# Differential attention in a two-layer hybrid block: where the difference of the two softmax maps is formed

## The chip, the cores and the metric

The kernel runs on one core of a Trainium2 chip. A core has five engines with queues of their own: TensorE (PE, matrix products into PSUM), VectorE (DVE), ScalarE (ACT, activations), GpSimd (POOL) and SyncE (SP, which issues the DMAs). Each engine takes its instructions strictly in the order in which they were written into its queue, and semaphores make them wait for one another. The metric is the device time of one execution in microseconds, the median of several runs.

## The reference

Two layers, each with three mixers side by side (neighbourhood attention, differential attention, a bidirectional state space model), an output projection, and a gated MLP with a convolution. The change touches differential attention alone. There are 4 heads, and each has two softmax maps, of which the second is taken off with a learned factor:

```python
def diff_attend(q, k, v, lam):
    s = jnp.einsum('bqhmd,bkhmd->bhmqk', q, k).astype(jnp.float32) * DF_HEAD_DIM ** -0.5
    p = jax.nn.softmax(s, axis=-1)
    a = p[:, :, 0] - lam * p[:, :, 1]
    return jnp.einsum('bhqk,bkhe->bqhe', a.astype(v.dtype), v)
```

Each output row of a head is then divided by its root mean square (`finish` in `diff_mixer`), so a common factor of a row drops out but for the small constant in that norm. 1024 latent tokens read 1280 keys (latent and context); in layer 0 the 256 context tokens are queries too and read the 256 context keys.

## The kernel before

All values are float32. The big projections split their operands into two float32r halves and use three products instead of one float32 product. Differential attention is the generator `df_stream` (L716). Its unit is 128 queries of one head: 40 units in layer 0 (of which 8 have 256 keys and the rest 1280) and 32 in layer 1, 72 in all. A unit has three steps.

`scores` (L743): for each of the two maps three float32r products of queries and keys into PSUM (L759; 512, 512 and 256 keys). DVE copies each out into the map's tile `e` and takes its maximum (L760), ACT applies the exponential with the row sum accumulated into `sums` (L764). The maps are not divided by their sums: the ratio rho = -lambda * sum0 / sum1 is formed (L767 on DVE, L768 on POOL), and POOL forms e0 + rho * e1 in two passes over 1280 columns (L770, L772).

`turn` (L778): PE transposes the result in blocks of 128 x 128 (L786), four of them into one PSUM bank, and ACT copies each bank into a tile `at` (L787). There are 10 blocks in a unit of 1280 keys, 656 in all.

`values` (L791): the transposed blocks are the moving side of the products with the values (L801), whose stationary side has 64 columns. Every fourth query tile the row norm follows (L812 to L827), and the result goes to DRAM in `ydd`.

The stream runs one unit ahead: `scores` of unit i stands in front of `turn` of unit i-1. Its first ten steps are interleaved with the projection of the neighbourhood values (`proj_tm`, L849), the rest with neighbourhood attention (`natt`, L1069) and with the modulation products of the next layer (`ada_native`, L325). The loop at L864 deals these out in proportion. On top of that a scheduler, which goes by its own estimate of how long things take, decides the order in each engine's queue when the program is built. The program text is therefore no guide to the order, and the tables below are.

After the stage the output projection (`outproj`, L1655) reads `ydd` back from DRAM.

In the names: `s` and `t` are PSUM tiles of scores and of transposed blocks, `qst` and `ks` queries and keys, `cs` the constants (with the identity in it), `dfv` the values, `o` the output in PSUM. Names with n in front (`ns`, `nt`, `nsb`, `npt`, `nk`, `nqs`) belong to neighbourhood attention.

Of the kernel before, what the change touches and what calls it, by code (L numbers as in the profile page):

```python
# [10 lines left out]
F32 = mybir.dt.float32  # L11
F32R = mybir.dt.float32r
ACTF = mybir.ActivationFunctionType
ALU = mybir.AluOpType
# [21 lines left out]
NB = 12  # L36
XN = (0, 0)
PD = 0
DG = lambda b, qt, hh: True

V_CW = 0
V_CB = V_CW + 40
# [38 lines left out]
def hybrid_kernel(ctx, tc, xin, cc, w_ada, bada, gmf, w_in, w_dt, w_out, w_up, w_dn, vec, cst, rope, nab, out):  # L81
    nc = tc.nc
    V, S, G, PE, SP = nc.vector, nc.scalar, nc.gpsimd, nc.tensor, nc.sync
# [49 lines left out]
    dr = ctx.enter_context(tc.tile_pool(name="dr", bufs=1, space=DRAM))  # L133
# [52 lines left out]
    ident = C(C_ID)  # L186
# [328 lines left out]
    def mixer(l):  # L515
# [9 lines left out]
        lam = keep.tile([128, 1], F32, name="lam")  # L525
# [62 lines left out]
        with phase(f"sw{l}") as sp:  # L588
          dte = sp.tile([128, NT, 16], F32, name="dte")
          tot = sp.tile([128, NT, 16], F32, name="tot")  # L590
          with phase(f"dtp{l}") as p:
# [13 lines left out]
            for t in range(NT):  # L605
                PE.matmul(pd_[:, t * 16:(t + 1) * 16], dt32[:, t * 128:(t + 1) * 128], C(C_I16, 16, 32),
                          start=True, stop=True)
            sm = lambda nm: p.tile([128, NT, 16], F32, name=nm)
            x0, ax, e, u, lu, um, eq = [sm(nm) for nm in ("sx", "sax", "se", "su", "slu", "sum_", "seq")]
            V.tensor_tensor(out=x0, in0=pd_[:, 0:160].rearrange("p (t c) -> p t c", t=NT),  # L610
                            in1=vc[:, l, V_DTB:V_DTB + 16].unsqueeze(1).to_broadcast([128, NT, 16]), op=ALU.add)
# [35 lines left out]
          if True:  # L647
            p = sp
# [67 lines left out]
        def df_stream():  # L716
            ks = {}
            units = [(b, qt, hh) for b in range(2) for qt in range(10 if full else 8) for hh in range(2)]
            held = {}
            qst = {}  # L720
            po = {}
            dgs = {}

            def load_k(b):
                t = (p if b == 0 else ksp[0]).tile([128, 4, T], F32R, tag="ks", name="ks")
                for j in range(4):
                    SP.dma_start(out=t[32 * j:32 * j + 32].bitcast(F32),
                                 in_=qkd[l][1, b, j // 2].rearrange("(m d) t -> d m t", m=4))
                ks[b] = t

            def load_q(b, qt):
                t = p.tile([128, 4, 128], F32R, tag="qst", name="qst", bufs=2)
                for j in range(4):
                    SP.dma_start(out=t[32 * j:32 * j + 32].bitcast(F32),
                                 in_=qkd[l][0, b, j % 2, :, qt * 128:qt * 128 + 128]
                                 .rearrange("(m d) t -> d m t", m=4))
                qst[b, qt] = t

            def keys(qt):
                k0, nk = (0, T) if qt < 8 else (SEQ, CTX)  # L740
                return k0, nk, [(c, min(512, nk - c)) for c in range(0, nk, 512)]

            def scores(b, qt, hh):  # L743
                if b not in ks:
                    load_k(b)
                if (b, qt) not in qst:
                    load_q(b, qt)
                k0, nk, kch = keys(qt)
                es = []
                if hh == 0 and qt % 4 == 0:  # L750
                    dgs[b, qt // 4] = p.tile([128, 2, 8], F32, tag="sums", name="sums", bufs=3)
                sm, u = dgs[b, qt // 4], qt % 4 * 2 + hh
                for m in range(2):
                    mi = hh * 2 + m
                    e = p.tile([128, T], F32, tag="e", name="e", bufs=EB)
                    mx = p.tile([128, 4], F32, tag="mx", name="mx", bufs=4)
                    for ci, (c, n) in enumerate(kch):
                        s_ = pst("s", 2)[:, :n]
                        PE.matmul(s_, qst[b, qt][:, mi], ks[b][:, mi, k0 + c:k0 + c + n], start=True, stop=True)  # L759
                        V.tensor_scalar(out=e[:, c:c + n], in0=s_, scalar1=1.0, scalar2=None,  # L760
                                        op0=ALU.mult, op1=ALU.max, accum_out=mx[:, ci:ci + 1])
                    nm = p.tile([128, 1], F32, tag="nm", name="nm", bufs=4)
                    V.tensor_reduce(out=nm, in_=mx[:, 0:len(kch)], axis=AX.X, op=ALU.max, negate=True)  # L763
                    act(out=e[:, 0:nk], in_=e[:, 0:nk], func=ACTF.Exp, bias=nm, accum_out=sm[:, m, u:u + 1])  # L764
                    es.append(e)
                rho = p.tile([128, 1], F32, tag="rho", name="rho", bufs=4)
                V.reciprocal(out=rho, in_=sm[:, 1, u:u + 1])  # L767
                G.tensor_scalar(out=rho, in0=rho, scalar1=sm[:, 0, u:u + 1], scalar2=lam, op0=ALU.mult, op1=ALU.mult)  # L768
                if DG(b, qt, hh):
                    G.tensor_scalar(out=es[1][:, 0:nk], in0=es[1][:, 0:nk], scalar1=rho, scalar2=1.0,  # L770
                                    op0=ALU.mult, op1=ALU.mult)
                    G.tensor_tensor(out=es[0][:, 0:nk], in0=es[0][:, 0:nk], in1=es[1][:, 0:nk], op=ALU.add)  # L772
                else:
                    V.scalar_tensor_tensor(out=es[0][:, 0:nk], in0=es[1][:, 0:nk], scalar=rho,
                                           in1=es[0][:, 0:nk], op0=ALU.mult, op1=ALU.add)
                held[b, qt, hh] = es[0]

            def turn(b, qt, hh):  # L778
                k0, nk, kch = keys(qt)
                e0 = held[b, qt, hh]  # L780
                ac = []
                for c, n in kch:
                    at = p.tile([128, n], F32, tag=f"at{n}", name="at", bufs=n // 128)
                    tp = pst("t", 2)
                    for i in range(n // 128):
                        PE.transpose(tp[:, i * 128:(i + 1) * 128], e0[:, c + i * 128:c + (i + 1) * 128], ident)  # L786
                    S.copy(out=at[:, :n], in_=tp[:, :n])  # L787
                    ac.append(at)
                held[b, qt, hh] = ac

            def values(b, qt):  # L791
                g0, gn = (qt // 4 * 4, 4) if qt < 8 else (8, 2)
                qi = qt - g0
                if qi == 0:
                    po[b] = pst("o", 1)
                k0, nk, kch = keys(qt)
                nkt = nk // 128
                for kt in range(nkt):
                    for hh in range(2):
                        hd = 2 * b + hh  # L800
                        PE.matmul(po[b][64 * hh:64 * hh + 64, qi * 128:(qi + 1) * 128],  # L801
                                  dfv[:, k0 // 128 + kt, hd * 64:(hd + 1) * 64],
                                  held[b, qt, hh][kt // 4][:, (kt % 4) * 128:(kt % 4 + 1) * 128],
                                  start=(kt == 0), stop=(kt == nkt - 1))
                if qi < gn - 1:
                    return
                n = gn * 128
                c0 = g0 * 128
                pv = po[b][:, :n]
                tl = lambda nm, dt=F32: p.tile([128, 512], dt, tag=nm, name=nm, bufs=1)[:, :n]  # L810
                sq, oh = tl("dsq"), tl("doh", F32R)
                act(out=sq, in_=pv, func=ACTF.Square)  # L812
                dg = p.tile([128, 8], F32, tag="dg", name="dg", bufs=2)
                s0 = dgs[b, qt // 4][:, 0, 0:2 * gn]
                V.scalar_tensor_tensor(out=dg[:, 0:2 * gn], in0=s0, scalar=64 * EPS, in1=s0, op0=ALU.mult, op1=ALU.mult)
                pm = pst("t", 2)[:, :n]
                PE.matmul(pm, C(C_BD64), sq, start=True, stop=False)
                for i in range(gn):
                    for hh in range(2):
                        PE.matmul(pm[64 * hh:64 * hh + 64, i * 128:(i + 1) * 128],  # L820
                                  dg[:, 2 * i + hh:2 * i + hh + 1].to_broadcast([128, 64]), ident,
                                  start=False, stop=(i == gn - 1))
                rstd(sq, pm, 1.0 / 64, oh.bitcast(F32), bias=0.0)
                V.scalar_tensor_tensor(out=sq, in0=pv, scalar=sub, in1=sq, op0=ALU.mult, op1=ALU.mult)
                split(oh, sq, sq, G)
                SP.dma_start(out=ydd[l][2 + b, 0, :, c0:c0 + n], in_=oh.bitcast(F32))
                SP.dma_start(out=ydd[l][2 + b, 1, :, c0:c0 + n], in_=sq)  # L827

            for i in range(len(units) + 1):
                if i < len(units):  # L830
                    scores(*units[i])
                if i > 0:
                    b, qt, hh = units[i - 1]
                    turn(b, qt, hh)
                    if hh:
                        values(b, qt)
                yield
# [1043 lines left out]
```

## Time and profile before

| | |
|---|---|
| three runs | 3574.5, 3579.18, 3580.07 us (median 3579.18) |
| the profiled execution | 3568.3 us, its span 3566.3 us |
| PE busy | 3274.8 us (92%), 17970 records |
| weight loads on PE | 2579.0 us (72%) |
| POOL busy | 1797.8 us (50%), 1391 instructions |
| DVE busy | 2272.8 us (64%) |
| ACT busy | 1514.2 us (42%) |

The differential stage of layer 0 lies at about 606 to 905 us of the span and that of layer 1 at about 2440 to 2730 us. A PE instruction shows as two kinds of record: a weight load (PEld, the stationary side) and a matmul (PE, the moving side). A transposition has one record of each kind (656 for 656 blocks), a float32 product has two of each (1312 of L801 for 656 products), a float32r product one. Successive matmuls overlap in the trace: one of 128 columns lasts some 270 ns, but the next starts much earlier. What an instruction costs PE is read from start to start, not from its duration.

### The profile page before, as it was taken

How to read it: one execution, taken by the hardware profiler on the slowest of the kernel's cores; microseconds unless marked ns; L12 is line 12 of the kernel's file. 1: busy time of each engine (PE TensorE's matmuls, PEld its weight loads, DVE VectorE, ACT ScalarE, POOL GpSimd, SP SyncE). 2: the span in 40 equal slices, each digit the busy share in tenths (PEclk: the TensorE clock that was granted, in tenths of full speed). 3: DMA queues.
4: the chain of work that ended last, by engine and by line, in shares of the span. 5: the costliest groups of instructions: out<-in, count | busy, mean ns of one | idle time of the engine just before them, and what ended most of it. 6: DMA issues, size and time to landing. Idle time of an engine off the chain costs nothing. (4 is left out here: it accounts for less than half of the span.)

```text
span 3566.3 us, 50227 instructions
## 1 busy us (share of the span) xinstructions
PE 3274.8 (92%) x17970; PEld 2579.0 (72%) x17970; DVE 2272.8 (64%) x4074; ACT 1514.2 (42%) x2641; POOL 1797.8 (50%) x1391
## 2 busy tenths in 40 slices
PE   7998998899888999998998998998998979999899
PEld 3876776667767887887786876776766757777677
DVE  6635875667485555556768745884674666776753
ACT  4233433778263233333335433344774533333343
POOL 2136663667244444544554226663674455555444
PEclk8999999999999999999999999998999989999999
DMA  8355444753722222225443245447555422222633
GB/s 294 105 189 180 133 124 134 193 153 107 260 90 68 89 91 79 89 86 183 145 133 110 84 145 198 125 131 190 169 172 194 152 71 89 92 93 99 240 114 118
DMA packets 328473, 491.24 MB, mean 138 GB/s; under 512 B 28320, under 2 KB 182048, under 8 KB 327968
## 3 DMA queue, kind: packets, MB, share of 16 engines
q1 hardware_dynamic: 328224, 488.03, 43.0%
q8 instruction: 142, 2.33, 0.3%
q14 instruction: 107, 0.88, 0.1%
HBM read 349.25 MB, written 138.67 MB: 137 GB/s over the span
## 5 line engine op out<-in xcount | busy, mean ns | idle before, releaser
L269 POOL TENSOR_TENSOR wL<-wr,wH 128x1024 fp32r<-128x1024 f32 x80 | 204.3, 2557 | 425.9 <-ACT wH L268 384.9
L1226 POOL TENSOR_TENSOR wL<-wr,wH 128x1024 fp32r<-128x1024 f32 (+1 forms) x102 | 229.5, 2252 | 339.5 <-ACT wH L1223 308.5
L760 DVE TENSOR_SCALAR_CACHE_REDUCE e<-s 128x512 f32<-128x512 f32 (+1 forms) x400 | 229.4, 590 | 140.9 <-PE s L759 135.6
L1226 POOL TENSOR_TENSOR wL<-wd,wH 128x512 fp32r<-128x512 f32 (+1 forms) x134 | 215.2, 1623 | 201.0 <-ACT wH L1223 200.6
L1226 POOL TENSOR_TENSOR wL<-ws,wH 128x512 fp32r<-128x512 f32 x168 | 254.1, 1532 | 111.8 <-ACT wH L1223 111.7
L1226 DVE TENSOR_TENSOR bL<-br,bH 128x512 fp32r<-128x512 f32 x154 | 145.4, 948 | 132.0 <-ACT bH L1223 131.0
L93 ACT ACTIVATE e<-e,nm 128x1280 f32<-128x1280 f32 (+1 forms) x144 | 183.3, 1273 | 41.6 <-DVE nm L763 34.4
L1223 ACT CAST wH<-wr 128x1024 fp32r<-128x1024 f32 (+1 forms) x102 | 91.8, 905 | 252.7 <-PE mm L1218 184.0
L1223 ACT CAST wH<-ws 128x512 fp32r<-128x512 f32 x168 | 98.0, 619 | 232.6 <-PE mm L1218 104.1
L772 POOL TENSOR_TENSOR e<-e 128x1280 f32<-128x1280 f32 (+1 forms) x72 | 193.0, 2682 | 3.9
L759 PE MATMUL s<-ks,qst 128*128 128x512 f32 (+1 forms) x400 | 164.5, 449 | 27.9 <-DMA qst<-qkd 13.9
L995 POOL TENSOR_SCALAR mf<-cs,lah 128x128 fp32r<-128x128 f32 x288 | 138.8, 498 | 51.6 <-PE s L997 50.9
L1373 DVE SCALAR_TENSOR_TENSOR fa<-fpad,vc,fa 128x1282 f32<-128x1282 f32 (+1 forms) x88 | 140.6, 1654 | 36.5 <-ACT fa L93 36.5
L1218 PE MATMUL A<-bL,wH 128*128 128x512 f32 x352 | 141.0, 400 | 12.0 <-DVE bL L1226 11.7
L1223 ACT CAST bH<-br 128x512 fp32r<-128x512 f32 x154 | 95.3, 619 | 125.5 <-DMA br<-hdd 55.6
L1223 ACT CAST wH<-wd 128x512 fp32r<-128x512 f32 (+1 forms) x134 | 86.7, 683 | 139.6 <-PE B L1218 70.3
L422 PE MATMUL mm<-h_0H,wH 128*128 128x512 f32 x320 | 135.0, 423 | 4.4 <-DVE aqs L690 3.1
L1219 PE MATMUL A<-bH,wL 128*128 128x512 f32 x352 | 137.6, 397 | 0.0
L423 PE MATMUL mm<-h_0L,wH 128*128 128x512 f32 x320 | 131.5, 411 | 1.9 <-DVE h_0L L402 1.9
L422 PE MATMUL mm<-h_1H,wH 128*128 128x512 f32 x320 | 131.4, 412 | 1.5 <-ACT z L93 1.5
L424 PE MATMUL mm<-h_1H,wL 128*128 128x512 f32 x320 | 130.3, 407 | 0.0
L424 PE MATMUL mm<-h_0H,wL 128*128 128x512 f32 x320 | 130.0, 406 | 0.0
(871 smaller groups left out, 10652.4 us busy)
## 6 DMA issues: line engine op xcount, KB each, us to landing
wr<-in_w_up_dram SPq DMA_DIRECT2D x94, 512.0 KB
br<-hdd SPq DMA_DIRECT2D x154, 256.0 KB
wa<-in_w_ada_dram SPq DMA_DIRECT2D x56, 512.0 KB
wr<-in_w_in_dram SPq DMA_DIRECT2D x48, 512.0 KB
hdd<-c SPq DMA_DIRECT2D x88, 256.0 KB
wr<-in_w_ada_dram SPq DMA_DIRECT2D x40, 512.0 KB
wd<-in_w_dn_dram SPq DMA_DIRECT2D x38, 512.0 KB
hdd<-fa SPq DMA_DIRECT2D x66, 256.0 KB
```

What stands on the lines that cost most here:

```text
L93: ins = S.activation(**kw)
L269: (eng or G).tensor_tensor(out=wl, in0=wr, in1=wh.bitcast(F32), op=ALU.subtract)
L422: PE.matmul(ps[:, :n], wh[:, ks], r, start=(i == 0), stop=False)
L424: PE.matmul(ps[:, :n], wl[:, ks], r, start=False, stop=(i == KT - 1))
L759: PE.matmul(s_, qst[b, qt][:, mi], ks[b][:, mi, k0 + c:k0 + c + n], start=True, stop=True)
L760: V.tensor_scalar(out=e[:, c:c + n], in0=s_, scalar1=1.0, scalar2=None, op0=ALU.mult, op1=ALU.max, accum_out=mx[:, ci:ci + 1])
L772: G.tensor_tensor(out=es[0][:, 0:nk], in0=es[0][:, 0:nk], in1=es[1][:, 0:nk], op=ALU.add)
L995: (V if hh % 2 else G).tensor_scalar(out=mf[:, hh], in0=C(mk), scalar1=lah[:, e, c, h:h + 1], scalar2=1.0, op0=ALU.mult, op1=ALU.mult)
L1218: PE.matmul(ps, wh, bl, start=False, stop=False, skip_group_check=True)
L1223: S.copy(out=out_h, in_=src)
L1226: le.tensor_tensor(out=out_l, in0=src, in1=out_h.bitcast(F32), op=ALU.subtract)
L1373: V.scalar_tensor_tensor(out=a[:, :W], in0=pads[r][:, j:j + W], scalar=vcol(l, fw + j), in1=a[:, :W], op0=ALU.mult, op1=ALU.add)
```

## The change

The two passes of POOL over the maps go. Instead, `turn` lets PE form the difference while it transposes: a product with the identity as the moving side puts the transposed block of e0 into PSUM, and a second product adds the block of e1 with a diagonal matrix as the moving side. On that diagonal stands rho for each query. The matrix `dr` (128 x 128) is made for each unit by one POOL instruction from `idl`, which is -lambda times the identity and is made once per layer on DVE.

```diff
@@ df_stream
             held = {}
+            idl = p.tile([128, 128], F32, name="idl")
+            V.tensor_scalar(out=idl, in0=ident, scalar1=lam, scalar2=1.0, op0=ALU.mult, op1=ALU.mult)
@@ scores
                 V.reciprocal(out=rho, in_=sm[:, 1, u:u + 1])
-                G.tensor_scalar(out=rho, in0=rho, scalar1=sm[:, 0, u:u + 1], scalar2=lam, op0=ALU.mult, op1=ALU.mult)
-                if DG(b, qt, hh):
-                    G.tensor_scalar(out=es[1][:, 0:nk], in0=es[1][:, 0:nk], scalar1=rho, scalar2=1.0,
-                                    op0=ALU.mult, op1=ALU.mult)
-                    G.tensor_tensor(out=es[0][:, 0:nk], in0=es[0][:, 0:nk], in1=es[1][:, 0:nk], op=ALU.add)
-                else:
...
-                held[b, qt, hh] = es[0]
+                dr_ = p.tile([128, 128], F32, tag="dr", name="dr", bufs=3)
+                G.tensor_scalar(out=dr_, in0=idl, scalar1=rho, scalar2=sm[:, 0, u:u + 1], op0=ALU.mult, op1=ALU.mult)
+                held[b, qt, hh] = es[0], es[1], dr_
@@ turn
-                e0 = held[b, qt, hh]
+                e0, e1, dr_ = held[b, qt, hh]
...
                     for i in range(n // 128):
-                        PE.transpose(tp[:, i * 128:(i + 1) * 128], e0[:, c + i * 128:c + (i + 1) * 128], ident)
+                        o, kb = slice(i * 128, (i + 1) * 128), slice(c + i * 128, c + (i + 1) * 128)
+                        PE.matmul(tp[:, o], e0[:, kb], ident, start=True, stop=False)
+                        PE.matmul(tp[:, o], e1[:, kb], dr_, start=False, stop=True)
```

`DG` was always true, so the `else` branch was never taken. Because the scheduler decides the order, the queues of the two stages are shuffled as well; outside of them they keep their order but for a few neighbours that swap places.

PE's queue in layer 0, from the row norm of the first four query tiles on, before (L817 and L820 are the norm, L786 the transpositions, L759 the scores, L1127, L1132 and L1153 neighbourhood attention):

```order
L817 MATMUL t<-dsq,cs 128x512
L820 MATMUL t<-cs,dg 64x128 x8
L786 MATMUL t<-cs,e 128x128 x4
L759 MATMUL s<-ks,qst 128x512
L1153 MATMUL nt<-cs,nsb 128x128
L759 MATMUL s<-ks,qst 128x256
L1127 MATMUL ns<-nk,nqs 128x384 x2
L1132 MATMUL ns<-nk,nqs 128x256 x2
L786 MATMUL t<-cs,e 128x128 x6
```

The same place in the changed kernel, where the lines are numbered a little differently (L814 and L817 the norm, L760 the scores, L782 the product with the identity, L783 the one with the diagonal):

```order
L814 MATMUL t<-dsq,cs 128x512
L817 MATMUL t<-cs,dg 64x128 x8
L760 MATMUL s<-ks,qst 128x256
L760 MATMUL s<-ks,qst 128x512
L782 MATMUL t<-cs,e 128x128
L783 MATMUL t<-dr,e 128x128
L782 MATMUL t<-cs,e 128x128
L783 MATMUL t<-dr,e 128x128
L782 MATMUL t<-cs,e 128x128
L783 MATMUL t<-dr,e 128x128
L782 MATMUL t<-cs,e 128x128
L783 MATMUL t<-dr,e 128x128
```

Where four transpositions stood in a row there now stand eight float32 products, each with a stationary block of 128 columns of its own; the scores of a later unit have moved ahead of them.

POOL's queue in the same stage, before (L768 makes rho, L770 and L772 the passes over the maps, L1141 belongs to neighbourhood attention):

```order
L768 TENSOR_SCALAR rho<-rho,sums,lam 128x1
L770 TENSOR_SCALAR e<-e,rho 128x1280
L1141 TENSOR_SCALAR nsb<-nsb,nsm 128x640
L772 TENSOR_TENSOR e<-e 128x1280
L1141 TENSOR_SCALAR nsb<-nsb,nsm 128x640
```

And in the changed kernel (L770 makes the diagonal matrix, L1138 is the former L1141, L281 the former L282):

```order
L770 TENSOR_SCALAR dr<-idl,rho,sums 128x128
L1138 TENSOR_SCALAR nsb<-nsb,nsm 128x640
L770 TENSOR_SCALAR dr<-idl,rho,sums 128x128
L281 TENSOR_TENSOR dsq<-dsq,doh 128x512
L770 TENSOR_SCALAR dr<-idl,rho,sums 128x128
```

Three instructions per unit, two of them over the whole width of the maps, have become one of 128 columns.

## Rows read from the trace of the kernel before

**Rows 1.** The page, busy time of each engine: us, share, instructions.

```profile
PE 3274.8 (92%) x17970; PEld 2579.0 (72%) x17970; DVE 2272.8 (64%) x4074; ACT 1514.2 (42%) x2641; POOL 1797.8 (50%) x1391
```

**Rows 2.** Layer 0 by stretches: from:to, length, PE, PEld, DVE, ACT, POOL; clock.

```profile
606.00:660.00 54.00, 45.71 (x307) 36.51 (x307) 28.67 (x115) 29.39 (x53) 26.97 (x19) 0.86 0.55 142
...
820.00:860.00 40.00, 39.47 (x346) 29.06 (x348) 30.53 (x131) 34.58 (x70) 31.61 (x23) 1.00 0.44 135
...
606.00:896.00 290.00, 268.76 (x2216) 201.78 (x2217) 191.84 (x808) 211.74 (x447) 194.80 (x161) 0.94 0.52 145
```

**Rows 3.** Layer 1 by stretches, the same columns.

```profile
2440.00:2520.00 80.00, 64.15 (x407) 45.44 (x405) 43.48 (x183) 44.61 (x80) 41.99 (x31) 0.79 0.78 199
...
2560.00:2600.00 40.00, 39.61 (x352) 29.25 (x350) 30.50 (x128) 33.33 (x70) 23.43 (x21) 1.00 0.50 150
...
2440.00:2722.00 282.00, 258.73 (x2135) 187.69 (x2135) 178.51 (x739) 197.43 (x388) 184.14 (x134) 0.93 0.57 159
```

**Rows 4.** PE in order of time, transpositions and values: start, length, line, count.

```profile
821.48 1.03 PE L786 MATMUL t<-cs,e 128*128 128x128 f32 x8
822.35 0.51 PE L309 MATMUL ns<-cs,arow 128*128 128x2 f32 x4
...
824.20 1.09 PE L801 MATMUL o<-at,dfv 128*64 128x128 f32 x16
825.22 0.51 PE L759 MATMUL s<-ks,qst 128*128 128x512 f32 x1
```

**Rows 5.** PE in order of time, two float32 products of 128 x 128.

```profile
335.37 0.60 PE L967 MATMUL s<-ux 128*128 128x128 f32 x4
```

**Rows 6.** PE in order of time, a float32 product with the identity, and the next.

```profile
2369.38 0.38 PE L1012 MATMUL o<-cs,yo 128*128 128x128 f32 x2
2369.59 0.39 PE L1039 MATMUL s<-yrs,cs 128*128 128x128 f32 x2
```

**Rows 7.** Groups by line on PE, whole span: busy, mean ns, idle before.

```profile
L801 PE MATMUL o<-at,dfv 128*64 128x128 f32 x1312 | 105.1, 289 | 0.6 <-DVE dsq L824 0.6
L786 PE MATMUL t<-cs,e 128*128 128x128 f32 x656 | 102.5, 286 | 1.0 <-POOL e L772 0.5 <-ACT doh L93 0.2
```

**Rows 8.** Groups by line on POOL, whole span.

```profile
L772 POOL TENSOR_TENSOR e<-e 128x1280 f32<-128x1280 f32 x64 | 187.2, 2926 | 3.6
L995 POOL TENSOR_SCALAR mf<-cs,lah 128x128 fp32r<-128x128 f32 x288 | 138.8, 498 | 51.6 <-PE s L997 50.9 <-POOL mf L995 0.5
L770 POOL TENSOR_SCALAR e<-e,rho 128x1280 f32<-128x1280 f32 x64 | 86.2, 1348 | 5.1
...
L768 POOL TENSOR_SCALAR rho<-rho,sums,lam 128x1 f32<-128x1 f32 x72 | 25.1, 349 | 142.1 <-DVE rho L767 80.3 <-DVE nm L763 37.6 <-PE s L759 7.6
...
L772 POOL TENSOR_TENSOR e<-e 128x256 f32<-128x256 f32 x8 | 5.8, 730 | 0.3
...
L770 POOL TENSOR_SCALAR e<-e,rho 128x256 f32<-128x256 f32 x8 | 3.8, 478 | 0.4
```

**Rows 9.** Waits in layer 0, 606 to 896 us: total us, times, longest.

```profile
PEld s L759 <- DVE e L760: 22.5, 56, 3.1
...
PE s L759 <- DMA qst<-qkd: 8.8, 2, 6.4
...
PE ns L1127 <- DMA nk<-nqd: 5.8, 2, 5.3
```

**Rows 10.** The end of layer 1's stage: POOL's last unit, and the output projection.

```profile
2707.54 0.33 POOL L768 TENSOR_SCALAR rho<-rho,sums,lam 128x1 f32<-128x1 f32 x1 [1.89 <-DVE rho L767]
2707.97 1.35 POOL L770 TENSOR_SCALAR e<-e,rho 128x1280 f32<-128x1280 f32 x1
...
2710.05 2.92 POOL L772 TENSOR_TENSOR e<-e 128x1280 f32<-128x1280 f32 x1
...
2733.57 1.50 PE L422 MATMUL mm<-T20H,wH 128*128 128x512 f32 x3 [4.70 <-DMA T20H<-ydd]
```

More of the change, by code (lines that the diff above doesn't have):

```diff
@@ L38 @@
 PD = 0
-DG = lambda b, qt, hh: True
 V_CW = 0
@@ L767, in scores @@
                 V.reciprocal(out=rho, in_=sm[:, 1, u:u + 1])
-                G.tensor_scalar(out=rho, in0=rho, scalar1=sm[:, 0, u:u + 1], scalar2=lam, op0=ALU.mult, op1=ALU.mult)
-                if DG(b, qt, hh):
-                    G.tensor_scalar(out=es[1][:, 0:nk], in0=es[1][:, 0:nk], scalar1=rho, scalar2=1.0,
-                                    op0=ALU.mult, op1=ALU.mult)
-                    G.tensor_tensor(out=es[0][:, 0:nk], in0=es[0][:, 0:nk], in1=es[1][:, 0:nk], op=ALU.add)
-                else:
-                    V.scalar_tensor_tensor(out=es[0][:, 0:nk], in0=es[1][:, 0:nk], scalar=rho,
-                                           in1=es[0][:, 0:nk], op0=ALU.mult, op1=ALU.add)
-                held[b, qt, hh] = es[0]
+                dr_ = p.tile([128, 128], F32, tag="dr", name="dr", bufs=3)
+                G.tensor_scalar(out=dr_, in0=idl, scalar1=rho, scalar2=sm[:, 0, u:u + 1], op0=ALU.mult, op1=ALU.mult)
+                held[b, qt, hh] = es[0], es[1], dr_
             def turn(b, qt, hh):
                 k0, nk, kch = keys(qt)
-                e0 = held[b, qt, hh]
+                e0, e1, dr_ = held[b, qt, hh]
                 ac = []
```

## The prediction

> **What bounds the kernel now.** I read the page first: PE is busy for 92% of the span and POOL for half [rows 1]. Such a share is a mean over many stages, so next I cut out the two stages that hold the lines of the change, 606 to 896 us and 2440 to 2722 us [rows 2, 3]. There PE is busy for 268.76 of 290 us and 258.73 of 282 us, and POOL, which the change relieves, for 194.80 and 184.14 us. A busy PE is not PE at its peak, since its records overlap. The weight loads tell more: PEld is busy for 201.78 and 187.69 us, 0.70 and 0.67 of the stage. In the two densest stretches PE does not pause at all (39.47 and 39.61 of 40 us), and yet PEld there reaches only 29.06 and 29.25 us, 0.73. The rest goes into changes between stationary blocks of 64 and of 128 columns and into short waits. So 0.73 is about what a bound PE shows in this mixture, and the stage as a whole stands at 0.70 and 0.67: PE is already the bound over most of both stages, and little of its time is free.
>
> The waits agree. The transpositions, which need what POOL makes, waited for its last pass for 0.5 us in all of the kernel [rows 7]. PE's larger waits in layer 0 are those of the scores for a free PSUM buffer (22.5 us in 56 pieces) and of first operands for DMAs at the start (8.8 and 5.8 us) [rows 9]. The change shortens none of these.
>
> **The change, part by part.**
>
> PE, removed: 656 transpositions [rows 7]. Eight of them start at 821.48 and the next instruction at 822.35 [rows 4]: 0.87 / 8 = 0.109 us each, 71 us in all.
>
> PE, added: 1312 float32 products with a stationary block of 128 columns and 128 moving columns. Two products of just that shape are the four records at 335.37 [rows 5]: 0.60 us, less one record's length of some 0.27 us that overlaps, over three steps is 0.11 us per record, 0.22 us per product. The product that is nearest in kind, with the identity on the moving side, starts at 2369.38 and the next starts at 2369.59 [rows 6]: 0.21 us. A block therefore costs 0.42 to 0.44 us in place of 0.109 us, 0.31 to 0.33 us more. Over 656 blocks that is 203 to 217 us; I take 210. A lower bound is the rate of L801: 16 records in 1.02 us [rows 4] are 0.064 us per record, which would give 656 x (4 x 0.064 - 0.109) = 96 us. Those have 64 stationary columns and alternate between two heads' halves of the array; the new products have 128, so I go by rows 5 and 6.
>
> Here a rule of the Trainium skill speaks still more strongly against the change. "TensorE: Matmul & The Clock Gate", section Terms, says that TensorE's transposition mode is four times faster for float32. By that rule a block would cost eight transpositions' time instead of four, and the added time would be 501 us. The rows say twice (0.21 or 0.22 against 0.109 us), and the sum goes by them; the rule is a rival below.
>
> What hides it: only time in which PE has nothing to do. If both stages became as dense as their densest stretch, they would take 201.78 / 0.727 = 278 and 187.69 / 0.727 = 258 us for today's work, so 12 + 24 = 36 us of the added work finds room. The ends are 0 (the new work stands in the queue behind the same waits) and 91 us, half of the 88 + 94 = 182 us in which no weight is being loaded, since part of that is the DMA waits at the start and the changes of width, which remain. I take 36, the end that dense stretches show.
>
> POOL: 64 x (1.348 + 2.926) + 8 x (0.478 + 0.730) + 72 x 0.349 = 308 us go, and 72 diagonals of 128 x 128 come, each about as long as L995, 0.498 us [rows 8]: 36 us. POOL loses 272 us of work off the path: nearly nobody waits for it, and what it still does in the stage is short. Its one place on the path is the end of layer 1, where the last unit runs through L768, L770 and L772 from 2707.54 to 2712.97 before its transpositions, and `ydd` is what the output projection waits for [rows 10]. With a diagonal in their place this is some 4 us shorter. In layer 0 neighbourhood attention ends last and nothing is gained. I take 4 us, between 0 and 5.
>
> DVE gets two instructions more in the whole kernel (`idl`), under a microsecond: nothing. ACT copies the same banks. The buffers of `e` are held until PE has read them, as before; e1 is held a little longer, but PE reads it in the same step as e0. No DMA is added, and SP's queue only changes its order within the stages.
>
> The added wait: the product with the diagonal waits for POOL in PE's strict order, and behind it stand scores and neighbourhood products. The turn comes a unit after the scores, so the diagonal should long be there; cost nothing, and the rival says what it is if not.
>
> The clock: 0.94 and 0.93 on average in the stages [rows 2, 3] mean that PE stood at 1.2 GHz for 12 and 14% of them, mostly at the start, where it waited. A PE with fewer pauses may win back up to half of that time, 17 + 20 us; I take it as part of the room above, not beside it.
>
> Sum: 210 - 36 - 4 = +170 us. Against the profiled execution (3568.3 us) that is 3738 us; that execution was 10.9 us below the median of the three runs, and against the median it is 3749. I forecast 3743 us; its own range is 3695 to 3796 (at the bottom the lower price, 203 us, twice the room and the profiled execution as base; at the top the higher price, 217 us, no room at all and the median as base).
>
> **The rivals.**
>
> *PE's gaps take most of it.* For it: 182 us without a weight load in the two stages. Against it: the dense stretches, where 0.73 was all. With 91 us of room: 210 - 91 - 4 = +115, 3683 to 3694 us.
>
> *Not slower: the paired products run at the pace of L801.* If the second product of a block overlaps with the first and a record costs 0.064 us, 96 us are added. It decides from the point at which the gaps take all of them: with 91 us of room and 4 us at the end, +1, about 3575 us; with more room it would be a gain, up to the 182 us that hold no weight load. Against it: every row with 128 stationary columns shows 0.105 us or more.
>
> *The diagonal is late.* If PE stands still for each unit while POOL makes the diagonal, one link as from L768 to L770 (0.43 us [rows 10]) and 0.498 us for the matrix, 72 x 0.93 = 67 us come on top: +237, 3805 to 3816 us. Against it: the unit's lead, and POOL's empty queue.
>
> *A float32 product costs four transpositions.* 501 - 40 = +461, about 4035 us. Against it: rows 5 and 6, which are the same shape.
>
> **How the numbers follow.** The forecast 0.70, gaps 0.15, not slower 0.04, late diagonal 0.08, fourfold price 0.03. The range 3670 to 3805 us holds the forecast and the gap case with some margin below it, and touches the late diagonal; it leaves out 0.11 to 0.15 and what of the first two lies beyond their bounds. A difference of 0.2%, 7 us, is about what can be told from no change. Only the third case can end there or below: faster 0.02, same 0.02, slower 0.96.
>
> **What would show it.** In the changed profile PE should have some 1970 records more and POOL about 270 us less busy time; the two stages should last about 85 us longer each, all the rest as long as before. Right: the pairs start 0.42 to 0.44 us apart in a run of blocks, and PE has hardly a wait for POOL. Wrong: pairs closer than 0.3 us, or stages in which PEld rises well above 0.75 (more room than I saw), or waits of the second product for `dr`.

## The result, and the profile after

The changed kernel takes 3769.3 us (median of 4 runs, 3764.83 to 3773.7) against 3578.93 us of the kernel before, run beside it (3574.5 to 3580.07): a ratio of 1.0536, with a 95% interval of 1.0514 to 1.0558. The change costs 190 us.

The page of the changed kernel, the line of engines as in [rows 1]:

```profile
PE 3492.8 (93%) x19938; PEld 2814.0 (75%) x19938; DVE 2284.0 (61%) x4076; ACT 1528.4 (41%) x2641; POOL 1513.6 (40%) x1247
```

PE has 1968 records and 218 us of busy time more, POOL 284 us less. In the changed kernel's timeline of PE (start, length, line, count) the pairs stand like this:

```profile
708.72 0.39 PE L782 MATMUL t<-cs,e 128*128 128x128 f32 x2
708.94 0.39 PE L783 MATMUL t<-dr,e 128*128 128x128 f32 x2
709.16 0.39 PE L782 MATMUL t<-cs,e 128*128 128x128 f32 x2
709.38 0.39 PE L783 MATMUL t<-dr,e 128*128 128x128 f32 x2
```

A product starts 0.22 us after the one before it, a pair 0.44 to 0.45 us after the pair before. A transposition took 0.109 us [rows 4]. So a block costs some 0.334 us more, and 656 blocks some 219 us.

To see where this goes, each stage is cut from its first score product to the first product of the output projection that waits for `ydd`. These are the two stages of the kernel before (from:to, length, then busy us and records of PE, PEld, DVE, ACT, POOL, then PE's granted clock):

```profile
606.10:919.77 313.67, 283.48 (x2322) 210.89 (x2322) 201.66 (x838) 221.65 (x476) 202.38 (x169) 0.94 0.52 147
...
2445.19:2733.57 288.38, 264.76 (x2179) 192.27 (x2179) 181.63 (x744) 200.13 (x394) 185.40 (x135) 0.94 0.56 159
```

and of the changed kernel:

```profile
612.48:1016.66 404.18, 387.55 (x3330) 325.83 (x3331) 199.90 (x838) 229.18 (x476) 61.04 (x89) 0.97 0.40 112
...
2557.69:2935.43 377.74, 363.51 (x3139) 301.56 (x3139) 184.81 (x744) 206.07 (x394) 52.13 (x71) 0.98 0.43 122
```

The stages grew by 90.5 and 89.4 us. Two columns show where the rest of the 219 us went. PE's pauses (length less busy) shrank from 53.8 to 30.9 us, and PE's busy time grew by 203 us only, while its granted clock rose from 0.94 to 0.97 and 0.98.

In the changed kernel DVE and ACT wait for PE, and POOL waits for DVE. The waits in layer 0 (total us, times, longest) have these among the largest:

```profile
POOL dr L770 <- DVE rho L768: 150.4, 22, 28.5
DVE e L761 <- PE s L760: 113.0, 88, 19.3
...
ACT at L784 <- PE t L783: 60.3, 46, 9.9
```

In the kernel before, PE's largest wait for another engine in layer 0 was that of the weight loads of the scores, for DVE to empty a PSUM bank: 22.5 us in 56 pieces [rows 9]. The same wait in the changed kernel:

```profile
PEld s L760 <- DVE e L761: 3.5, 11, 0.6
```

The product with the diagonal hardly ever waits for POOL: 0.8 us in the whole kernel, and a diagonal takes 0.453 us. The groups of the changed kernel (busy, mean ns, idle before):

```profile
L783 PE MATMUL t<-dr,e 128*128 128x128 f32 x1312 | 252.8, 279 | 0.9 <-POOL dr L770 0.8
...
L770 POOL TENSOR_SCALAR dr<-idl,rho,sums 128x128 f32<-128x128 f32 x72 | 32.6, 453 | 383.0 <-DVE rho L768 243.7
```

The end of layer 1's stage, POOL's last diagonal and PE's first product of `ydd`, as in [rows 10]:

```profile
2909.30 0.44 POOL L770 TENSOR_SCALAR dr<-idl,rho,sums 128x128 f32<-128x128 f32 x1 [2.08 <-DVE rho L768]
```

```profile
2935.43 0.80 PE L421 MATMUL mm<-T20H,wH 128*128 128x512 f32 x1 [4.47 <-DMA T20H<-ydd]
```

From one to the other 26.1 us; before, from L768 on, 26.0 us. Nothing was gained at the end: the diagonal was ready at 2909.74, but PE was still busy with older work.

### The profile page after: what moved, and what is told of

Same layout as the page of the kernel before. It is cut to its first block, busy times and chain, and to the rows that moved or that the text cites. A ratio compares the mean times of both kernels' runs of the same rounds, so it can differ in the third digit from the quotient of the medians.

```text
span 3771.2 us, 53893 instructions
## 1 busy us (share of the span) xinstructions
PE 3492.8 (93%) x19938; PEld 2814.0 (75%) x19938; DVE 2284.0 (61%) x4076; ACT 1528.4 (41%) x2641; POOL 1513.6 (40%) x1247
## 5 line engine op out<-in xcount | busy, mean ns | idle before, releaser
L761 DVE TENSOR_SCALAR_CACHE_REDUCE e<-s 128x512 f32<-128x512 f32 (+1 forms) x400 | 231.3, 593 | 235.3 <-PE s L760 229.7
L782 PE MATMUL t<-cs,e 128*128 128x128 f32 x1312 | 260.0, 281 | 0.0
L783 PE MATMUL t<-dr,e 128*128 128x128 f32 x1312 | 252.8, 279 | 0.9 <-POOL dr L770 0.8
L782 PEld LDWEIGHTS t<-cs,e 128*128 128x128 f32 x1312 | 207.8, 194 | 15.9 <-issue 9.2
L783 PEld LDWEIGHTS t<-dr,e 128*128 128x128 f32 x1312 | 204.0, 194 | 6.4 <-issue 2.2
L770 POOL TENSOR_SCALAR dr<-idl,rho,sums 128x128 f32<-128x128 f32 x72 | 32.6, 453 | 383.0 <-DVE rho L768 243.7
L760 PE MATMUL s<-ks,qst 128*128 128x512 f32 (+1 forms) x400 | 163.6, 434 | 17.6 <-DMA qst<-qkd 15.6
L1138 POOL TENSOR_SCALAR nsb<-nsb,nsm 128x640 f32<-128x640 f32 (+1 forms) x72 | 55.0, 765 | 256.5 <-DVE nsm L1137 156.0
L784 ACT COPY at<-t 128x512 f32<-128x512 f32 (+1 forms) x200 | 100.0, 503 | 112.5 <-PE t L783 110.3
```

The source lines that it names most:

```text
L782: PE.matmul(tp[:, o], e0[:, kb], ident, start=True, stop=False)
L783: PE.matmul(tp[:, o], e1[:, kb], dr_, start=False, stop=True)
```

## The experiments

Twelve kernels were run. This table has what the texts below rest on, read from the same cut of both stages: their length, PE's busy time and pauses in them, PE's granted clock in layer 0 and 1, and the median time with its ratio to the kernel before. "Added" is the extra PE work at the pace of the timelines (0.109 us a transposition, 0.222 us a float32 product, 0.11 us a float32r product). Each ratio is taken to the kernel before as it ran beside that kernel (medians of 3572.61 to 3578.93 us), and the differences in the texts likewise.

| kernel | added | stages | PE busy | pauses | clock | median, ratio |
|---|---|---|---|---|---|---|
| before, two profiles | 0 | 602.1, 596.5 | 548.2, 539.0 | 53.8, 57.6 | .94 .94, .95 .95 | 3578.93 |
| after, two profiles | 219 | 781.9, 781.0 | 751.1, 750.6 | 30.9, 30.4 | .97 .98, .97 .98 | 3769.3, 1.0536 |
| one product | 74 | 648.5 | 615.3 | 33.2 | .98 .96 | 3616.71, 1.0122 |
| POOL and product | 74 | 666.9 | 611.5 | 55.4 | .95 .95 | 3639.0, 1.0191 |
| turned twice | 72 | 676.6 | 617.9 | 58.7 | .95 .93 | 3643.43, 1.0205 |
| pair in float32r | 73 | 672.6 | 631.4 | 41.2 | .95 .91 | 3657.42, 1.0238 |
| three products | 365 | 897.7 | 879.4 | 18.3 | .99 .99 | 3870.24, 1.0831 |
| fixed diagonal | 219 | 772.6 | 746.0 | 26.6 | .98 .98 | 3748.88, 1.0504 |
| difference on DVE | 0 | 645.2 | 563.6 | 81.7 | .91 .91 | 3615.51, 1.0122 |
| half on DVE | 0 | 604.6 | 546.6 | 57.9 | .96 .93 | 3573.83, 1.0002 |
| lag of two | 0 | 605.0 | 546.7 | 58.3 | .94 .94 | 3574.95, 1.0003 |
| norm off DVE | 0 | 602.1 | 544.1 | 57.9 | .94 .93 | 3575.11, 1.0001 |

**One product.** The changed kernel with the identity product alone; the second map is left out of the result.

```diff
-    PE.matmul(tp[:, o], e0[:, kb], ident, start=True, stop=False)
-    PE.matmul(tp[:, o], e1[:, kb], dr_, start=False, stop=True)
+    PE.matmul(tp[:, o], e0[:, kb], ident, start=True, stop=True)
```

> The changed kernel without the product with the diagonal: one float32 product per block, the second map is left out of the result. PE's work is 656 x (0.222 - 0.109) = 74 us above the kernel before, and POOL is relieved. Theory (PE is the bound; its added time is paid but for a fixed room of about 37 us that the first added work fills): +37 us against before, about 3616. Rival 1 (a share of 0.82 of any added PE time is paid, 180 of 219): +61, about 3640. Rival 2 (the cost is the new order of the queues or the wait for the diagonal, not PE's time): about +0, or as slow as the changed kernel, 3769.

Measured +44 us (interval 1.0104 to 1.014), nearer to the theory's 37 than to the rival's 61. This fits a room of some 30 us. But see the next one.

**POOL and product.** The kernel before, with the same product in place of the transposition.

```diff
-    PE.transpose(tp[:, o], e0[:, kb], ident)
+    PE.matmul(tp[:, o], e0[:, kb], ident, start=True, stop=True)
```

> The kernel before, its difference still formed by POOL, with each transposition replaced by one float32 product with the identity: the same PE work as with one product, POOL as loaded as before. Theory: POOL's relief is worth at most 4 us, so within 5 us of the one-product kernel (+37, 3616; by rival 1 +61, 3640). Rival 3 (POOL's relief hides part of the price of the products in the changed kernel): 20 us or more slower than the one-product kernel.

Measured +66 us (1.0169 to 1.0212), 22 us more than one product, with the same work on PE. POOL's two passes are there as well, and the queues come out in another order. The stages of POOL and product:

```profile
609.67:954.57 344.90, 317.92 (x2658) 250.82 (x2658) 203.50 (x838) 224.56 (x476) 202.38 (x169) 0.95 0.46 131
...
2494.38:2816.38 322.00, 293.61 (x2499) 229.18 (x2499) 193.01 (x744) 202.76 (x394) 184.41 (x135) 0.95 0.52 143
```

and of one product:

```profile
607.31:937.62 330.31, 315.91 (x2658) 246.44 (x2658) 193.92 (x838) 223.87 (x476) 61.01 (x89) 0.98 0.49 139
...
2469.62:2787.82 318.20, 299.41 (x2498) 229.99 (x2498) 179.20 (x744) 202.75 (x394) 52.01 (x71) 0.96 0.52 144
```

PE is equally busy (611.5 and 615.3 us); its pauses are 55.4 us with POOL's passes and 33.2 us without. A part of the difference belongs to the scores, which wait for DVE to empty a PSUM bank. The group of their loads in POOL and product:

```profile
L759 PEld LDWEIGHTS s<-ks,qst 128*128 128x128 f32 x400 | 74.3, 199 | 65.1 <-DVE e L760 30.2 <-issue 28.2 <-DVE nm L763 1.6
```

and of one product:

```profile
L760 PEld LDWEIGHTS s<-ks,qst 128*128 128x128 f32 x400 | 72.3, 192 | 53.7 <-issue 26.5 <-DVE e L761 17.6 <-DVE rho L768 2.4
```

The larger part is something else. PE's waits in both stages, the last one for `ydd` included and summed by what ended them, are 44.8 us for DMAs and 15.1 us for DVE in POOL and product, and 30.2 and 8.0 us in one product. So about two thirds of the 22 us of pauses stand before DMAs. The longest single wait in POOL and product, 10.4 us in layer 1, is one for weights of the modulation products:

```profile
PE ns L344 <- DMA wa<-in_w_ada_dram: 10.6, 2, 10.4
```

By their medians the two kernels differ by 22 us. That POOL's load makes this difference, and not the new order of the queues, is not shown.

**Turned twice.** The kernel before, each transposition issued twice.

```diff
+    PE.transpose(tp[:, o], e0[:, kb], ident)
     PE.transpose(tp[:, o], e0[:, kb], ident)
```

> The kernel before with each transposition issued twice to the same place (the first result is overwritten), GpSimd's passes kept; the added TensorE work is 656 x 0.109 = 72 us of transpositions. Theory (the added TensorE time is paid for but for some room, and GpSimd's passes stay on the path): as with the f32 product that costs the same 72 us, +60 to +68 us. Rival (the stage has a fixed 39 us of room): +33 us.

Measured +69 us (1.0186 to 1.0223), with 58.7 us of pauses. Added PE work of 72 us is paid for nearly in full while POOL keeps its passes: the rival's fixed room of 39 us does not exist. This was just above the expected 60 to 68.

**Three products.** The changed kernel with the identity product issued twice.

```diff
+    PE.matmul(tp[:, o], e0[:, kb], ident, start=True, stop=True)
     PE.matmul(tp[:, o], e0[:, kb], ident, start=True, stop=False)
```

> The changed kernel with the product with the identity issued twice (the first result is overwritten): 656 x 0.222 = 146 us more PE work than the changed kernel, 365 us more than before. Theory (fixed room, already filled): +146 against the changed kernel, about 3915. Rival 1 (a share of 0.82): +120, about 3889. Rival 2 (order or wait): the changed kernel's time within 20 us.

Measured 101 us above the changed kernel (by the ratios 105) for 146 us of products (1.081 to 1.0851 against before), less than both of my figures, 146 and 120. The stages:

```profile
613.32:1076.50 463.18, 454.97 (x4002) 395.82 (x4002) 202.63 (x838) 230.20 (x476) 61.76 (x89) 0.99 0.35 98
...
2609.47:3043.97 434.50, 424.46 (x3779) 368.76 (x3779) 187.26 (x744) 206.99 (x394) 52.35 (x71) 0.99 0.37 106
```

They are 116 us longer than those of the changed kernel; PE's pauses fall by 13 us more and the clock stands at 0.99. From the kernel before over the changed one to this one, PE pauses less (54, 31 and 18 us) and runs more of the stage at 2.4 GHz. It is no general rule: turned twice and the pair in float32r added work and show 0.91 to 0.95. What is missing between 116 and 101 lies outside the stages and was not traced to a cause.

**Pair in float32r.** The changed kernel with the maps, the identity and the diagonal as float32r, so that a product is one record.

```diff
-    e = p.tile([128, T], F32, ...)
+    e = p.tile([128, T], F32R, ...)
...
-    dr_ = p.tile([128, 128], F32, ...)
+    dr_ = p.tile([128, 128], F32R, ...)
...
-    PE.matmul(tp[:, o], e0[:, kb], ident, start=True, stop=False)
+    PE.matmul(tp[:, o], e0[:, kb], idr, start=True, stop=False)
```

> The changed kernel with both products of a block in float32r (maps, identity and diagonal rounded to float32r; less exact): one PE record per product instead of two. Estimate from the spacing of records, 0.11 us each: 656 x (0.22 - 0.109) = 73 us above before. Theory: the price hangs on the number of records, so two float32r products cost what one float32 product costs: +37, about 3616 (rival 1: +61, 3640). If it is the pair, the diagonal or the order that costs, and not the records: as slow as the changed kernel, 3769.

Measured +85 us (1.0221 to 1.0255). The price falls from 190 us, but it lies 41 us above one product, which adds as much to PE, and both of my figures (+37 and +61) missed. In the profiles the two kernels lie 34 us apart, and 24 of these in the stages: 16 us more of PE's busy time and 8 us more of pauses. POOL's passes are gone here too, and still the kernel is slower than POOL and product (+66), which has them. The windows at the start of layer 1, float32r pair:

```profile
2480.00:2490.00 10.00, 5.31 (x43) 5.13 (x43) 0.00 (x0) 0.00 (x0) 0.00 (x0) 0.91 0.89 183
2490.00:2500.00 10.00, 9.41 (x30) 6.68 (x29) 6.95 (x26) 5.48 (x9) 0.45 (x1) 0.50 0.46 139
2500.00:2510.00 10.00, 9.53 (x37) 8.29 (x38) 3.84 (x16) 5.36 (x9) 0.45 (x1) 0.50 0.35 101
```

For 20 us PE is granted 0.50, that is 1.2 GHz, after a stretch in which it was busy for half of the time; it gets 30 and 37 records done there against some 90 later. Over the stage the clock is 0.91, against 0.96 for one product. Work done at the lower clock fits PE's extra busy time. That float32r itself brings the lower clock is not shown, and the rest of the 41 us stays open.

**Fixed diagonal.** The changed kernel with `idl` in place of `dr`, and no diagonal made, so that the second map goes in without its ratio of sums.

```diff
-    G.tensor_scalar(out=dr_, in0=idl, scalar1=rho, scalar2=sm[:, 0, u:u + 1], ...)
...
-    PE.matmul(tp[:, o], e1[:, kb], dr_, start=False, stop=True)
+    PE.matmul(tp[:, o], e1[:, kb], idl, start=False, stop=True)
```

> The changed kernel with the diagonal product taken against the constant lambda-scaled identity; the per-unit diagonal matrix on GpSimd is left out, and with it the weight of the second map. TensorE's work is that of the changed kernel; GpSimd has nothing left in the chain. Theory (TensorE's added time sets the stage, the diagonal is always early): within 6 us of the changed kernel's 3769. Rival (part of the added time is a wait for the diagonal matrix or for the reciprocal before it): 10 to 40 us faster than it.

Measured 3748.88 us: 20 us below the changed kernel by the medians, 11 us by the ratios. The two intervals (1.0484 to 1.0525 and 1.0514 to 1.0558) just overlap. In the stages the difference is 9 us (5 busy, 4 pauses). So making and awaiting the diagonal costs some 10 of 182 us, at the edge of what these runs can tell: above the 6 us of my theory, and at the lower end of the rival.

**Difference on DVE, and half of it.** The kernel before with one DVE pass in place of POOL's two, for all units or for every second.

```diff
-DG = lambda b, qt, hh: True
+DG = lambda b, qt, hh: False        # half: hh == 0
```

> The kernel before with the difference of the maps formed by VectorE in one pass (scalar_tensor_tensor) in place of GpSimd's two; TensorE's work is that of before. If relieving GpSimd is worth about 20 us in itself (theory, from one product with and without GpSimd's passes: 44 and 66 us), and VectorE has the room for 72 passes of about 1.1 us (80 us in stages of 602 us, where it stands at about 0.57 to 0.65), the kernel is faster than before: 3552 to 3565 us. If GpSimd's passes cost nothing as long as TensorE sets the pace (rival: my prediction had 4 us), it stays within 5 us of before. If VectorE's added pass delays the evacuation of the scores, on which TensorE waits, it is slower: +10 to +40 us.

> As the kernel with the difference on VectorE, but for every second unit only (hh = 0); the other units keep GpSimd's two passes. Theory (GpSimd's load costs some 20 us): about half of that is gained, 3560 to 3572 us, and more than the whole move if VectorE is the next engine to be late. Rival (GpSimd's passes cost nothing): within 4 us of before.

Measured +41 us (1.0105 to 1.0138) and no difference (0.9988 to 1.0015). The groups of the difference on DVE:

```profile
L786 PE MATMUL t<-cs,e 128*128 128x128 f32 x656 | 107.2, 294 | 18.5 <-DVE e L774 15.4 <-ACT e L93 1.2 <-ACT at L787 1.1
L774 DVE SCALAR_TENSOR_TENSOR e<-e,rho 128x1280 f32<-128x1280 f32 (+1 forms) x72 | 106.1, 1473 | 10.7 <-POOL rho L768 10.7
```

The pass takes 1.47 us, the transpositions now wait for it (15.4 us; for POOL it was 0.5 us [rows 7]), and PE pauses for 81.7 us. My expectation of a gain failed. The time is that of the third case, at its upper end, but its mechanism, a delay of the scores' way out, does not show. The loads of the scores wait for DVE about as long as in the kernel before, 32.6 against 38.0 us in both stages; here they are in layer 1, first before and then with the difference on DVE:

```profile
PEld s L759 <- DVE e L760: 15.5, 41, 1.0
```

```profile
PEld s L759 <- DVE e L760: 17.0, 44, 1.1
```

What grew by 28 us are PE's pauses as a whole: its waits for DVE by 14 us, which the transpositions account for, and its waits for DMAs by 12 us. With half of the units on DVE nothing was gained or lost. A relief of POOL and a load on DVE may cancel there, and the run doesn't tell them apart.

**Lag of two.** The kernel before with the transpositions two units behind the scores in the text.

```diff
-            for i in range(len(units) + 1):
+            for i in range(len(units) + 2):
...
-                if i > 0:
-                    b, qt, hh = units[i - 1]
+                if i > 1:
+                    b, qt, hh = units[i - 2]
```

> The kernel before with the transpositions and the value products two units behind the scores in the program text instead of one; all arithmetic, all instructions and GpSimd's passes are those of before. In the two stages of before TensorE idles 54 us, and 33 us where GpSimd's passes are gone. Theory (GpSimd's passes cost some 20 us because the transpositions of a unit come due before its difference is ready, and scores stall behind them): with twice the lead TensorE's idle time falls towards 33 us and the time to about 3555 us. Rival (the scheduler that orders the queues has its own idea of the lead, or the six score tiles, all in use at that lead, hold up the next scores): within 6 us of before or up to 20 us slower.

Measured no difference (0.9991 to 1.0015), with 58.3 us of pauses. The rival's time came, but the run says nothing on the lead, for the lead did not change. In layer 1 a unit's first transposition starts 13.9 us after its last score product, on average over the 32 units, and 13.5 us in the kernel before; when it starts, the scores of one further unit have as a rule been issued, in both kernels. The scheduler shuffled the queue but put the lead back, so whether the lead is what POOL's passes cost stays untested.

**Norm off DVE.** In the kernel before some DVE instructions are stretched while POOL makes a pass. The longest one is `dg`, a square of 128 x 8 numbers. DVE in order of time:

```profile
666.26 2.71 DVE L815 SCALAR_TENSOR_TENSOR dg<-sums 128x8 f32<-128x8 f32 x1
...
812.64 1.29 DVE L815 SCALAR_TENSOR_TENSOR dg<-sums 128x8 f32<-128x8 f32 x1
```

and POOL at the same times:

```profile
666.02 2.92 POOL L772 TENSOR_TENSOR e<-e 128x1280 f32<-128x1280 f32 x1
...
810.99 2.92 POOL L772 TENSOR_TENSOR e<-e 128x1280 f32<-128x1280 f32 x1
```

Both times `dg` ends with POOL's pass (at 668.97 and 668.94, at 813.93 and 813.91). All of it before (minimum, median and maximum ns):

```profile
L815 DVE SCALAR_TENSOR_TENSOR dg<-sums x10: 161/836/2708, 666.3 to 2703.4; 128x8 f32<-128x8 f32 x8, 128x4 f32<-128x4 f32 x2
```

and after:

```profile
L812 DVE SCALAR_TENSOR_TENSOR dg<-sums x10: 155/165/169, 683.0 to 2904.0; 128x8 f32<-128x8 f32 x8, 128x4 f32<-128x4 f32 x2
```

This was a further candidate for the 22 us, so the norm's instructions of this kind were moved to ACT and POOL:

```diff
-    V.scalar_tensor_tensor(out=dg[:, 0:2 * gn], in0=s0, scalar=64 * EPS, in1=s0, ...)
+    act(out=dg[:, 0:2 * gn], in_=s0, func=ACTF.Square, scale=(64 * EPS) ** 0.5)
...
-    rstd(sq, pm, 1.0 / 64, oh.bitcast(F32), bias=0.0)
+    rstd(sq, pm, 1.0 / 64, oh.bitcast(F32), bias=0.0, eng=G)   # refinement on POOL
```

> The kernel before with the two-operand VectorE instructions of the row norm taken off VectorE: the squares of the sums go to ScalarE, the refinement of the inverse root to GpSimd (three products and one scale-and-add, some 35 us more for GpSimd in all). GpSimd's two passes over the maps stay. In the profile of before these VectorE instructions are stretched while such a pass runs (the one of 128x8 takes 1.34 us on average and up to 2.71, against 0.165 where the passes are gone), some 17 us in all, and the scores wait for VectorE behind them. Theory (this hold is how GpSimd's passes come onto the path): TensorE's waits for VectorE shrink and the time falls by 8 to 17 us, to 3558 to 3567 us. Rival (the hold is a sign of the passes but not what costs, or the longer GpSimd queue costs as much): within 5 us of before.

Measured no difference (0.9988 to 1.0015): DVE is 28 us less busy in the stages, and PE's pauses are what they were (57.9 us). So taking the hold away gained nothing. POOL became 35 us busier by it in the stages, and whether that cost what the move saved, as the rival has it, the run can't tell.

**Both kernels again**, for a second profile.

> The changed kernel once more, for a second profile. If the split of the price (TensorE busy +203 us in the two stages, idle -23 us, granted clock 0.97 to 0.98 there against 0.94) belongs to the kernel, it comes out within 5 us and 0.01 again; the stretches outside the stages may differ from the first profile by some 10 us.

> The kernel before once more, for a second profile. The two stages again take 602 us with 54 us of TensorE idle at a granted clock of 0.94, within 5 us and 0.01; outside them some 10 us of difference would be no surprise.

After again:

```profile
603.81:1009.10 405.29, 387.90 (x3330) 326.74 (x3331) 199.92 (x838) 229.10 (x476) 61.36 (x89) 0.97 0.40 112
...
2549.53:2925.21 375.68, 362.68 (x3139) 300.25 (x3139) 184.64 (x744) 206.18 (x394) 52.40 (x71) 0.98 0.43 122
```

Before again:

```profile
610.46:919.56 309.10, 279.28 (x2323) 207.48 (x2323) 201.28 (x838) 221.75 (x476) 202.76 (x169) 0.95 0.52 149
...
2453.50:2740.95 287.45, 259.68 (x2178) 188.82 (x2178) 181.42 (x744) 200.16 (x394) 185.76 (x135) 0.95 0.56 159
```

After repeats within 1 us; before within 6 us in length and 9 us in PE's busy time. Differences below 10 us in a single profile therefore carry no weight here. Outside the stages the two profiles of before take 2964 and 2976 us and those of after 2989 and 2983 us; the other ten kernels, whose edits lie in the stages, take 2966 to 2982 us.

No version beat both kernels; three equalled the kernel before.

## Why the prediction was right, point by point

The mean of two profiles each gives the sum: the stages grew from 599.3 to 781.4 us, by 182 us, where the prediction had 170. PE's busy time grew by 207 us, and its pauses shrank by 25 us.

- *PE's price.* Predicted 203 to 217 us, taken as 210; the pace measured gives 219, just beyond the upper end. The mechanism and both rows [rows 5, 6] were right; the slower one, 0.11 us per record, was the one to take. The rule in the Trainium skill ("TensorE: Matmul & The Clock Gate", Terms: transposition mode four times faster for float32) does not hold for this pair of instructions: 0.222 against 0.109 us is twice.
- *The room.* Predicted 36 us, and 219 - 182 = 37 us did not have to be paid. The size was right and the reason was wrong, so the agreement is luck. I took it from the share of weight loads in dense stretches. What the runs show is 25 us of pauses that went, and 12 us between PE's work at full pace and its busy time. The pauses that went are waits for DVE above all: PE's waits for it in both stages fell from 17.0 to 2.5 us (19.2 to 2.6 in the second profiles), those for ACT from 5.0 to 0.6 us, those for DMAs by 3 to 4 us only. The clock accounts for the 12 us: a mean of 0.945 over 599 us is 66 us at 1.2 GHz, and 0.975 over 781 us is 39 us; half of that is lost, so 33 against 20 us at most. I had the clock in this term, as a part of it, and there it was right. No run changed the clock alone, so this part is worked out, not shown by an experiment.
- *The waits that stay.* Of PE's larger waits, the scores' for a free PSUM buffer and those for DMAs, the prediction says that the change shortens none. For the scores this step failed: 22.5 us in layer 0 became 3.5 us. Over both stages the wait is 38.0 us before, 30.2 us with one product added beside POOL's passes, 17.6 us with that product and no passes, and 7.0 us in the changed kernel. So it shrinks with the work added to PE, and at the same work the kernel without the passes has less of it.
- *POOL off the path.* Predicted: nearly nobody waits for it, 4 us at most. Direct waits for POOL are indeed few. But with equal PE work the kernel with POOL's passes took 22 us more than the one without them, so 4 us is not shown to be an upper bound. Nor is 22 us shown to be POOL's price: most of the longer pauses stand before DMAs, the queues also come out in another order without the passes, and no run separated the order from the load. Against the order speaks that lag of two and norm off DVE shuffled the queues too and kept the time; against the load, that the pair in float32r has no passes either and took 85 us for the same added work, more than the 66 us with them. How much POOL's relief is worth in the changed kernel stays open.
- *The end of layer 1.* Predicted -4 us, measured 0: PE was late, not POOL.
- *The late diagonal.* Rightly a rival with a small chance: 0.8 us of waits, and stages 9 us shorter where no diagonal is made.
- *What would show it.* Pairs 0.44 to 0.45 us apart, hardly a wait for `dr`, 1968 records and stages 90 us longer each: as told. But PEld rose well above 0.75, which I had given as a sign of more room. The windows of the changed kernel in layer 0, the dense stretch and the stage:

```profile
860.00:960.00 100.00, 100.00 (x914) 85.52 (x906) 53.41 (x221) 59.31 (x116) 16.65 (x22) 1.00 0.32 98
...
612.00:1003.00 391.00, 377.70 (x3281) 319.90 (x3282) 195.89 (x824) 223.43 (x460) 57.05 (x85) 0.98 0.40 111
```

  A dense stretch now shows 0.86 where it showed 0.73 [rows 2]. The added products follow one another with the same width of the stationary side, so I take it that the mixture changed and not the room; the sign was badly chosen.
- *The rest as long as before.* Outside the stages the mean is 16 us longer, where two profiles of one kernel differ by up to 11; 182 + 16 = 198 in the profiles, 190 in the medians. Why is open. The forecast of 3743 us came out 26 us short: 6 us because the kernel before ran at 3579 us and not at 3573, 9 us by PE's price, 4 us by the end of layer 1, and the rest outside the stages.

## What to carry to other kernels

Price an added PE instruction from start to start in a row of its own shape, and where PE bounds the stage expect to pay most of it, here 182 of 219 us. What comes off is pauses, and time at the lower clock; look at both columns of the stage's windows, and not at the share of weight loads. Whether an engine costs anything can't be read from direct waits for it alone: run the same PE work with and without its load, and look which waits differ. Where a scheduler orders the queues, read from the trace whether an edit changed what it was meant to change. And work moved off one engine can come back as a wait for another: here the transpositions waited 15 us for DVE's pass, where they had waited 0.5 us for POOL's.

## What the runs showed of the hardware that was not expected

A wait of some microseconds costs PE more than its length. In the changed kernel PE waits 6.7 us for `nk`, and then the products come at half the pace until 855.5 us:

```profile
850.06 0.98 PE L1124 MATMUL ns<-nk,nqs 128*128 128x384 f32 x2 [6.66 <-DMA nk<-nqd]
850.84 0.63 PE L783 MATMUL t<-dr,e 128*128 128x128 f32 x2
851.26 0.63 PE L782 MATMUL t<-cs,e 128*128 128x128 f32 x2
...
855.92 0.39 PE L782 MATMUL t<-cs,e 128*128 128x128 f32 x2
856.14 0.39 PE L783 MATMUL t<-dr,e 128*128 128x128 f32 x2
```

The windows of the wait and of the products after it, with the granted clock as the third number from the end:

```profile
843.00:850.00 7.00, 0.40 (x3) 0.16 (x2) 1.04 (x4) 1.16 (x2) 0.56 (x2) 0.67 1.03 219
850.00:855.50 5.50, 5.44 (x24) 5.47 (x25) 0.93 (x4) 0.59 (x1) 0.00 (x0) 0.50 0.41 106
```

0.42 us a product, then 0.22: in the wait the granted clock had fallen to 1.2 GHz, and the first products after it ran at that.

A DVE instruction that reads two operands in SBUF can stand until a pass of POOL ends: `dg` took up to 2.71 us where 0.16 is its own length. DVE's way out of PSUM was not stretched: the copy out of PSUM (L760, in the changed kernel L761) took 590 ns on average before, and 593 ns after, where the passes are gone.
